# One transformer trunk layer on one core: softmax reciprocals spread as two fp16 parts, some weight high parts on GpSimd, and another written order of the attention stage

## The chip, the core and the metric

The kernel runs on one NeuronCore of one Trainium2 chip. A core has a matrix engine (TensorE, PE in the profile), a vector engine (VectorE, DVE), an activation engine (ScalarE, ACT), a general engine (GpSimd, POOL) and a queue engine that issues transfers (SyncE, SP). Each engine executes its own queue of instructions in order, and engines wait for one another through semaphores. The metric is device time in microseconds of one execution of the whole program; lower is better.

## The reference, cut to what matters

One trunk layer is computed for 128 context tokens and 512 latent tokens, with shared weights. All arithmetic of the reference is float32. Only the attention core is touched by the change:

```python
def block_attention(q, k, v):          # N queries, 16 heads of 64, 4 key/value heads
    ...
    s = jnp.einsum('bqkgd,btkd->bkgqt', qblk, k).astype(jnp.float32) * scale
    p = jax.nn.softmax(s, axis=-1).astype(v.dtype)
    return jnp.einsum('bkgqt,btkd->bqkgd', p, v)

def mixer(u, p, rope_tabs, ctx_k, ctx_v):
    z = u @ p["w_in"]
    ...                                 # split; RMS-normalise q and k per head, rotate latent ones
    att = block_attention(q_used, keys, vals) @ p["w_att_out"]
    conv = (b_gate * dwconv3(c_gate * x_in, p["conv_w"])) @ p["w_conv_out"]
    merged = jax.nn.sigmoid(g_att) * att + jax.nn.sigmoid(g_conv) * conv
    return merged @ p["w_o"], k, v
```

Context queries see the 128 context keys. Latent queries see 640 keys: 128 cached ones and the 512 latent ones. After the mixer come a residual with a norm, and a feed-forward part with 2 x 2816 columns.

## The kernel before

The program has a first part (modulation vectors, normalisation, key and value projections), the attention stage, and then the long dense products (attention output, gates, convolution mixer, feed-forward). Nearly all products are made from split operands: a matrix is cut into a high part and a low part, and three products (high by high, high by low, low by high) are summed. The high part of a weight block of 128 x 1024 is a copy on ACT (work `hi u`, L825), the low part is the difference of the block and its high part, in two halves of 512 columns on DVE or POOL (work `lo u`, L830).

The attention stage is what the change touches. It is not written as a loop. Its Python code first makes a list of works, small groups of instructions on one engine with the works they depend on and the buffers they need. Then `follow(PLAN)` emits them in the order of a long table of numbers. An item such as `67a0` says: work 67, its first way of being done (`a`; `b` and `c` are the same work on another engine), and buffer 0 for the buffer that it must choose. So the table sets the order of every engine's queue, which engine does a work that has two ways, and which buffer is used. Nothing is decided while the program runs; an engine whose next instruction is not ready waits, and all behind it wait too.

The works are these, with the lines under which the profile shows them:

- Query tiles. There are 20 of them, for 4 key/value groups `g` and 5 token tiles `t` (tile 0 is the context). A tile is projected in four pieces `q.0` to `q.3` on PE, each of six matmuls of 256 columns (L708). Then it is rotated on DVE (L848, L849; for the context L844), added on POOL or DVE (L869), squared on ACT (L871) and summed on DVE (L873); a factor is made by a power on POOL (L876) and applied on POOL (L891); PE turns it (L1033), and ACT and DVE cut it (L1035, L1037). Keys go through the same steps (L881, L920, L926, L929).
- Steps. There are 36: for each of the 4 groups one step of the context tile with four heads, and two steps for each of the four latent tiles, with two heads each. A latent step `n` consists of `s` (12 matmuls of scores on PE, L1072); for each of its two heads a maximum on DVE (`max`, L1119), for the second head a shift by a constant on DVE (L1122), the exponential with its row sum on ACT (`exp`, L1127), the fp16 high part of the result on ACT (`P1`, L1133), its low part on DVE or POOL (`P2`, L1138, L1140) and a transposing transfer issued by SP (`T`, L1144); a reciprocal of the two row sums on DVE (`inv`, L1146); and `pv` on PE. The work `pv` first spreads the reciprocals over a PSUM bank by an fp32 product with the identity (L1161, one matmul for each head, a row of 128 reciprocals repeated 64 times) and then multiplies values by probabilities (L1169, 30 matmuls of fp16).
- After the two `pv` of a tile: `R` copies the spread reciprocals to SBUF on ACT (L1181), `O` multiplies on DVE by these and by a factor of the value columns (L1185), and `AH` and `AL` cut the result for the next product (ACT L1188, DVE L1191).
- Gates: `gate0` and `gate1` on PE (L708 too), the last of them after the last scores.

The scores of a head lie in one of three PSUM areas. Where the string `POOL_WAY` has a 1 for a step, the exponential of its second head goes to an SBUF buffer `E` (two of them) and the low part is made on POOL; otherwise it stays in its PSUM area until DVE has made the low part.

The attention stage lies from about 57 to 229 us in the profile: its first matmuls of L708 start at 56.91, the first of the next product (L235, tile b) at 229.02.

Of the kernel before, what the change touches and what calls it, by code (L numbers as in the profile page):

```python
# [26 lines left out]
HD = 64  # L27
# [23 lines left out]
67a0 44a0 12a00 203a 24a1 137a 34a2 68a 25a 13a 0a 32a11 131a 2a1 69a 11a 26a 6a 3a 41a 33b 70a 14a1 35a 51a2 4a 1a3 79a1 53a4  # L51
71a0 15a 21a 80a 36a 5b0 31a 72a2 81a 45a 52a3 7a 16a 37b1 82a 22a12 92a2 46a 85a1 73a 8a0 23b 83a10 17a2 54a3 9a 86a 132a 38a1
10a 27a3 42a01 18a0 39a 93a 55a 19a 43a 40a 28a4 74a 60b2 94a 29a 59b3 95a 87a 75b 20a 105a3 98a0 84a 30a 76a1 106a 88a 77a0 99a
78a 107a 100a 58b4 56a0 47b4 65a 347a2 57a 134b 61a 96a22 48a1 63a 348a 108a 97a 49a 118a0 349a 101a 109a01 119a 133b 50a 89a2
102a1 120a 62a 90a1 209a 111a2 351a1 91a 110a 121a 112a 138a 66a 113a 359a10 352a 124a1 103a2 114a 122a10 204a 353a5 365a 140b
115a4 135a0 116a3 366a 104a 367a0 139b 136a 117a 350a 360a 368a0 373a20 123a 275a 125a 361a 64a 126a 141a 362a4 379a 205b 142a
380a 371a 363a 381a1 354a1 369a 143a2 364a0 382a2 374a 391a10 355a2 144a0 356a 383a 375a 151a0 370a1 145a 397a 357a 152a 376a1
146a 398a 385a 384a2 392a 399a0 153a 377a 147a 393a 154a 358a 206b 405a02 394a3 378a3 155a01 400a4 395a 127a 148a1 157a2 411a
401a 149a0 128a3 372a0 396a4 129a1 412a 158a 413a1 130a 159a 406a 414a0 423a12 403a 402a5 150a 407a 415a 164a1 429a 408a2 165a
156a 430a 281a 409a 431a0 166a 416a0 160a 424a 432a1 167a 417a 425a 433a 437a02 168a20 426a3 435a 386a 170a1 443a 169a 410a1  # L60
444a 427a 177a1 387a2 445a1 388a 178a 438a 389a 428a2 446a4 455a12 390a 171a 439a 447a 404a0 456a 440a0 434a3 449a 457a 441a
172a 418a 461a 458a2 173a 161a2 442a4 419a1 179a 459a 162a2 180a 163a 462a 420a 463a0 469a10 448a5 181a10 464a3 467a 182a 487a2
470a 183a0 421a 465a 190a1 460a0 488a 471a 191a 475a 472a1 192a 422a 210a 184a 466a1 174a0 473a 193a 185a 175a3 489a 176a 476a
186a 194a02 450a0 211a 436a 212a 477a1 474a4 490a 195a 478a0 481a 499a10 196a2 907a 479a 451a1 197a 207a1 491a4 505a 276a 208a
198a 506a 480a5 452a 507a0 492a 213a 199a 500a 453a 513a20 508a2 493a2 454a 278b 501a 468a0 514a 509a 502a3 519a 515a 214a 503a
277b 510a3 516a1 482a 520a 215a2 521a1 517a 187a3 504a0 483a0 511a 525a 531a02 188a1 484a 522a0 189a 518a1 200a3 216a1 523a 537a
485a 494a1 201a0 486a 538a 217a 223a0 495a2 202a 524a4 218a 539a0 496a 224a 532a 497a 219a 540a4 545a12 498a 533a 911a 541a
220a1 551a 534a2 225a 221a2 552a 226a 535a 542a5 553a1 546a 554a3 563a02 227a11 547a 555a 536a2 222a 548a1 557a 512a1 569a 229a0
228a 570a 549a 571a0 526a 556a0 564a 572a0 577a12 543a 230a 527a0 573a 565a 528a 550a3 236a0 583a 529a 566a4 231a 237a 575a 584a
# [19 lines left out]
880a0 885a 934a 840a 856a0 841a 895a 886a5 896a 842a 935a2 897a 890a 898a1 936a 891a 899a 937a 892a4 901a 900a2 938a 943a 893a  # L89
939a 894a4 940a 870a 888a1 871a2 872a 902a 873a 874a 941a 903a1 904a 942a 905a 906a  # L90
"""
POOL_WAY = "11111111111111111111111101111100"


def rope_tables():
# [17 lines left out]
def trunk_layer(ctx, tc, x_prompt, x_sample, cache_k, cache_v, c, c_ctx, w_ada, b_ada, g_pre1, g_post1, g_pre2,  # L113
# [632 lines left out]
    with tc.tile_pool(name="att", bufs=1) as at:  # L746
# [45 lines left out]
        def at_bank(room, n=512):  # L792
            return bank_of(room.at[0][1])[:, 0:n]
# [1594 lines left out]
```

## Time and profile before

| what | value |
|---|---|
| median of three runs | 1079.62 us (1079.02 to 1079.99) |
| the profiled execution's own time | 1079.34 us |
| its span in the profile | 1077.5 us |
| PE, DVE, ACT, POOL busy, whole span | 1062.8, 870.3, 583.1, 130.8 us |
| attention stage | 57 to 229 us |

"Busy" is time in which an engine has an instruction in flight. Instructions of one engine overlap a little, so the time from the start of one to the start of the next is often shorter than the duration that a row shows; for the queue of an engine it is the start-to-start time that counts. A row of a group reads: line, engine, operation, output<-inputs, shape, count | busy time, mean duration in ns | idle time of the engine before these instructions, and what ended it. A row of a timeline reads: start, busy time, engine, line, operation, count, and in brackets the idle time before with what ended it.

### The profile page before, as it was taken

To read this page: it belongs to the slowest core of one execution; us is meant where nothing else is said; L and a number is where in the kernel's file an instruction comes from. 1 tells how busy PE (TensorE), PEld (TensorE's weight loads), DVE (VectorE), ACT (ScalarE), POOL (GpSimd) and SP (SyncE) were. 2 spreads that over 40 slices of the span, in tenths; PEclk is the share of its full clock that TensorE was granted. 3 is DMA by queue.
4 is the path that set the end of the run, shared out by engine and by line. 5 is a ranking of instruction groups with operands and counts; after the bars stand their busy time and mean duration, and the time that the engine had idled before them with its cause. 6 is when DMAs were issued, how large, how long until landed. Compare 5 with 4: busy or idle time off the path is not lost.

```text
span 1077.5 us, 20246 instructions
## 1 busy us (share of the span) xinstructions
PE 1062.8 (99%) x8066; PEld 992.2 (92%) x8066; DVE 870.3 (81%) x1328; ACT 583.1 (54%) x1050; POOL 130.8 (12%) x162
## 2 busy tenths in 40 slices
PE   8999999999999999999999999999999999999997
PEld 6788898899999999999998789999999999998886
DVE  5699899855498999896599678889998998989544
ACT  5478999942344554445322466655555654555432
POOL 1087676500000000000000020000000000000001
PEclk9999999999999999999999999999999999999999
DMA  9829999962244333233667634333443443326722
GB/s 316 260 80 175 190 172 180 194 144 60 78 123 124 98 94 94 79 89 100 184 191 257 196 122 137 111 103 104 130 134 112 130 127 106 116 91 210 266 77 98
DMA packets 238444, 152.17 MB, mean 141 GB/s; under 512 B 94602, under 2 KB 215942, under 8 KB 238350
## 3 DMA queue, kind: packets, MB, share of 16 engines
q1 hardware_dynamic: 238238, 150.84, 51.6%
q8 instruction: 63, 1.03, 0.4%
q14 instruction: 31, 0.25, 0.1%
q10 hardware_dynamic: 112, 0.04, 0.0%
HBM read 117.39 MB, written 11.44 MB: 120 GB/s over the span
## 4 chain that ended last, share of the span: by engine, by line
PE 89%; DVE 3%; DMA 3%; ACT 2%; POOL 1%; issue 1%; SPq 0%; DVEq 0%; ACTq 0%; POOLq 0%
PE b L1273 47%; PE b L235 10%; PE b L237 10%; PE b L236 10%; PE s L708 3%; PE s L1072 2%; PE s L1169 2%; DMA araw<-in_w_ada_dram 1%; DMA PT<-P 1%; PE s L235 1%; PE s L237 1%; PE s L477 1%; DMA XT<-in_w_ada_dram 1%; DVE marks L1119 1%; ACT P L1133 1%
## 5 line engine op out<-in xcount | busy, mean ns | idle before, releaser
L1273 PE MATMUL b<-ZBr,whi 128*128 128x320 f32 x688 | 152.2, 309 | 0.0
L1273 PE MATMUL b<-MT,whi 128*128 128x320 f32 x608 | 134.3, 308 | 0.0
L1273 PEld LDWEIGHTS b<-ZBr,whi 128*128 128x128 f32 x688 | 115.0, 188 | 0.1
L1273 PE MATMUL b<-ZBr,wlo 128*128 128x320 f32 x344 | 106.2, 309 | 0.0
L1273 PEld LDWEIGHTS b<-MT,whi 128*128 128x128 f32 x608 | 101.6, 187 | 0.0
L1273 PE MATMUL b<-MT,wlo 128*128 128x320 f32 x304 | 93.6, 308 | 0.0
L1260 ACT ACTIVATE whi<-SUM 128x1024 fp32r<-128x1024 f32 x40 | 42.2, 1055 | 78.4 <-DVE SUM L1812 75.9
L1842 DVE SCALAR_TENSOR_TENSOR Y<-C,cffn,Y 128x642 f32<-128x642 f32 x88 | 77.6, 881 | 0.9
L201 DVE TENSOR_TENSOR wlo<-raw,whi 128x1024 fp32r<-128x1024 f32 (+1 forms) x31 | 34.2, 1102 | 48.2 <-ACT whi L200 47.8
L1273 PE MATMUL b<-ZBT,whi 128*128 128x320 f32 x320 | 71.0, 309 | 0.0
L1273 PE MATMUL b<-UL,whi 128*128 128x320 f32 x228 | 70.7, 310 | 0.0
L1273 PE MATMUL b<-UH,wlo 128*128 128x320 f32 x228 | 70.1, 307 | 0.0
L1260 ACT ACTIVATE whi<-WB 128x1024 fp32r<-128x1024 f32 x38 | 40.1, 1055 | 55.3 <-DVE WB L1367 55.3
L1273 PE MATMUL b<-UH,whi 128*128 128x320 f32 x228 | 69.8, 306 | 0.0
L1273 PEld LDWEIGHTS b<-ZBr,wlo 128*128 128x128 f32 x344 | 64.6, 188 | 0.0
L1281 ACT ACTIVATE p<-b 128x320 f32<-128x320 f32 x78 | 34.2, 438 | 55.5 <-PE b L1273 53.7
L1264 DVE TENSOR_TENSOR wlo<-raw,whi 128x1024 fp32r<-128x1024 f32 (+1 forms) x51 | 50.3, 1017 | 10.3 <-ACT whi L1260 10.3
L1273 PEld LDWEIGHTS b<-MT,wlo 128*128 128x128 f32 x304 | 57.0, 187 | 0.0
L1273 PEld LDWEIGHTS b<-ZBT,whi 128*128 128x128 f32 x320 | 54.2, 188 | 1.5
L1119 DVE TENSOR_REDUCE marks<-s 128x1 f32<-128x640 f32 x64 | 52.0, 816 | 4.1 <-PE s L1072 3.8
L1264 DVE TENSOR_TENSOR wlo<-WB,whi 128x1024 fp32r<-128x1024 f32 x38 | 46.4, 1222 | 8.7 <-ACT whi L1260 8.6
L2250 POOL TENSOR_TENSOR ssqs<-ssqs 128x1 f32<-128x1 f32 x4 | 0.8, 194 | 417.2 <-ACT JK L2243 417.2
(424 smaller groups left out, 3256.8 us busy)
## 6 DMA issues: line engine op xcount, KB each, us to landing
raw<-in_w_in_dram SPq DMA_DIRECT2D x48, 512.0 KB
RAW<-in_w_up_dram SPq DMA_DIRECT2D x40, 512.0 KB
raw<-in_w_down_dram SPq DMA_DIRECT2D x22, 512.0 KB
GA<-in_w_ada_dram SPq DMA_DIRECT2D x16, 512.0 KB
actd<-Y SPq DMA_DIRECT2D x18, 321.0 KB
XT<-in_w_ada_dram SPq DMA_DIRECT2D x9, 512.0 KB
raw<-in_w_att_out_dram SPq DMA_DIRECT2D x8, 512.0 KB
raw<-in_w_conv_out_dram SPq DMA_DIRECT2D x8, 512.0 KB
```

Source lines behind the costliest of these rows:

```text
L201: V.tensor_tensor(out=lo[:, :n], in0=raw, in1=hi[:, :n].bitcast(F32), op=ALU.subtract)
L235: PE.matmul(out, ah, bh, start=start, stop=False)
L236: PE.matmul(out, ah, bl, start=False, stop=False)
L237: PE.matmul(out, al, bh, start=False, stop=stop)
L708: PE.matmul(out, a, b, start=start and n == 0, stop=stop and n == 2, skip_group_check=True)
L1072: PE.matmul(o[h], q_of(hl, i, rows), kk[kx][rows, g, ks], start=m == 0, stop=m == 2, tile_position=(64 * h, 0), skip_group_check=True)
L1119: V.tensor_reduce(out=mk[:, h:h + 1], in_=s_of(), axis=AX.X, op=ALU.max, negate=True)
L1260: S.activation(to[0], raw, AF.Copy)
L1264: V.tensor_tensor(out=lo, in0=raw, in1=hi.bitcast(F32), op=ALU.subtract)
L1273: PE.matmul(out, p[:, ws], q[:, k, :], start=start and k == 0 and n == 0, stop=stop and k == 3 and n == 2, skip_group_check=True)
L1281: S.activation(t, pair[j][b], AF.Copy)
L1842: V.scalar_tensor_tensor(out=y, in0=crows(j)[i][:, d:d + NACT], scalar=cffn[:, 44 * d + o:44 * d + o + 1], in1=y, op0=ALU.mult, op1=ALU.add)
```

## The change

It has three parts.

1. The reciprocal spread. `inv` stays on DVE. Three small works follow it for each step, each on DVE or POOL as the table says: `ri` multiplies the two (context tile: four) reciprocals by a power of two, `rh` casts them to fp16 in a new tile `shares`, `rl` writes the rest as a second fp16 value. `pv` spreads them by two fp16 products with an fp16 identity for each head, summed in PSUM, where it had one fp32 product. The factor of the value columns becomes the same for both heads, so its tile `vcol` has four columns.
2. `hi u` gets a second way: on POOL, as a product with a column of ones. The table takes it for the weight blocks 16 and 17.
3. A new table `PLAN` (1052 items, before 944; 108 of them are new works) and a new `POOL_WAY` (30 steps with their low part on POOL, before 29; the last four latent steps before were 1100 and are 1111 now).

By the two tables the works with two ways are divided so:

| work | before | after |
|---|---|---|
| `ri`, `rh`, `rl` (36 each) | none | 14, 17, 16 on DVE; 22, 19, 20 on POOL |
| `hi` of a weight block | 9 on ACT | 7 on ACT, 2 on POOL |
| `lo` (half a block) | 5 DVE, 13 POOL | 7 DVE, 11 POOL |
| `P2` of latent steps | 35 DVE, 29 POOL | 34 DVE, 30 POOL |
| `add` of keys and queries | 4 DVE, 16 POOL | 5 DVE, 15 POOL |
| `norm` of keys | 3 DVE, 2 POOL | 1 DVE, 4 POOL |
| `v lo` | 3 DVE | 2 DVE, 1 POOL |

All other works stay on their engines. The counts of matmuls of the stage, of transfers and of the works of `max`, `exp` and `P1` do not change, but for the spread.

The diff, cut:

```diff
 PLAN = """
-67a0 44a0 12a00 203a 24a1 137a 34a2 68a 25a 13a 0a 32a11 131a 2a1 69a ...
+67a0 44a0 32a00 131a 14a1 203a 68a 12a11 24a2 33a 31a 137a 21a 25a 69a ...
 """
-POOL_WAY = "11111111111111111111111101111100"
+POOL_WAY = "10111111111111110111111111111111"
...
-        some = at.tile([128, 128], BF16, name="some")
+        lifts = at.tile([128, 4], F32, name="lifts")
+        some = at.tile([128, 2], BF16, name="some")
+        ident16 = at.tile([128, 128], F16, name="ident16")
+        shares = at.tile([128, 8, 8], F16, name="shares")
         G.memset(some, 1.0)
-        for i in range(2):
-            G.tensor_scalar(out=backs[:, i:i + 1], in0=ident[:, 0:1], scalar1=2.0 ** (SHIFT * i), scalar2=None, op0=ALU.mult)
+        G.memset(lifts, 2.0 ** (2 * SHIFT))
+        G.memset(lifts[:, 0:1], 2.0 ** SHIFT)
+        G.tensor_copy(ident16, ident)
+        G.tensor_scalar(out=backs, in0=ident[:, 0:2], scalar1=2.0 ** (2 * SHIFT), scalar2=None, op0=ALU.mult)
...
-                S.activation(made["x"][1], raw, AF.Copy)
+                if eng is S:
+                    S.activation(made["x"][1], raw, AF.Copy)
+                else:
+                    G.tensor_tensor(out=made["x"][1], in0=raw, in1=ones[:, 0:1].broadcast_to((128, 1024)), op=ALU.mult)
...
+        def parted(n, m, lift, mk, after):
+            sh = shares[:, n % 8, :]
+
+            def small(eng):
+                eng.tensor_copy(sh[:, 0:m], mk[:, 8:8 + m])
+
+            def rest(eng):
+                eng.tensor_tensor(out=sh[:, 4:4 + m], in0=mk[:, 8:8 + m], in1=sh[:, 0:m], op=ALU.subtract)
+            def lifted(eng):
+                eng.tensor_tensor(out=mk[:, 8:8 + m], in0=mk[:, 8:8 + m], in1=lift, op=ALU.mult)
+            a = work(f"inv{n}", "DVE", lambda: V.reciprocal(mk[:, 8:8 + m], mk[:, 4:4 + m]), after)
+            a = also(work(f"ri{n}", "DVE", lambda: lifted(V), [a]), "POOL", lambda: lifted(G))
+            a = also(work(f"rh{n}", "DVE", lambda: small(V), [a]), "POOL", lambda: small(G))
+            return also(work(f"rl{n}", "DVE", lambda: rest(V), [a]), "POOL", lambda: rest(G))
...
-                invs = [work(f"inv{n}", "DVE", lambda mk=mk: V.reciprocal(mk[:, 8:10], mk[:, 4:6]), exs)]
+                invs = [parted(n, 2, lifts[:, 0:2], mk, exs)]
...
                     for h in range(2):
-                        c = 8 + 2 * i + h if t == 0 else 8 + h
-                        PE.matmul(p[64 * h:64 * h + 64, 256 + 128 * i:384 + 128 * i], mk[:, c:c + 1].broadcast_to((128, 64)), ident,
-                                  start=True, stop=True, tile_position=(0, 64 * h), skip_group_check=True)
+                        for m in range(2):
+                            c = 4 * m + (2 * i + h if t == 0 else h)
+                            PE.matmul(p[64 * h:64 * h + 64, 256 + 128 * i:384 + 128 * i], sh[:, c:c + 1].broadcast_to((128, 64)), ident16,
+                                      start=m == 0, stop=m == 1, tile_position=(0, 64 * h), skip_group_check=True)
```

The order itself is shown at two places on which the prediction rests. The first is PE at an ordinary `pv`, a latent step. Before, the spread is one row of two fp32 matmuls (L1161; `marks` holds the reciprocals) ahead of the value products (L1169, with values `VV` and transposed probabilities `PT`):

```order
L1072 MATMUL s2_103_932<-KH_167,QT1_765 128x320
L1161 MATMUL s1_94_786<-ident_72,marks_771 64x128 x2
L1169 LDWEIGHTS VV_171
L1169 MATMUL s1_94_786<-PT4_753,VV_171 64x128
L1169 MATMUL s1_94_786<-PT5_754,VV_171 64x128
```

and of the change the same place, where the spread (L1191, the pair of rows stands four times: high and low part of the first head, then of the second) is of fp16, with its weights loaded from `shares`:

```order
L713 MATMUL s1_98_843<-whi_99_861,UL_95 128x256
L1191 LDWEIGHTS shares_778
L1191 MATMUL s1_94_791<-ident16_777,shares_778 64x128
L1199 LDWEIGHTS VV_171
L1199 MATMUL s1_94_791<-PT3_752,VV_171 64x128
L1199 MATMUL s1_94_791<-PT2_751,VV_171 64x128
```

The fp32 spread of two matmuls became four matmuls of fp16, and what stands behind it is the same.

The second place is the POOL queue around the steps 15 to 19 (`P` rows are the low parts of the second heads; `rq` rows are factors; `QF` rows add and norm; `wlo` rows low parts of weights). Before:

```order
L1138 TENSOR_TENSOR P1_745<-E0_742,P1_745 128x640
L1138 TENSOR_TENSOR P2_746<-E1_743,P2_746 128x640
L876 TENSOR_TENSOR rq_768<-ssqs_770,mhalf_81 128x4
L891 TENSOR_TENSOR QF2_763<-QF2_763,rq_768 128x256
L830 TENSOR_TENSOR wlo_118_2409<-raw_110_1343,whi_117_2408 128x512
L869 TENSOR_TENSOR QF1_762<-QF1_762,X1_759 128x256
L1138 TENSOR_TENSOR P1_745<-E0_742,P1_745 128x640
```

and of the change (L1167 are the low parts of the second heads, L890 a factor, L843 half a low part of weights, L1075, L1070 and L1073 are `ri`, `rh` and `rl`, L838 is the high part of weight block 16):

```order
L1167 TENSOR_TENSOR P3_747<-E0_742,P3_747 128x640
L843 TENSOR_TENSOR wlo_118_2257<-raw_110_1307,whi_117_2256 128x512
L1075 TENSOR_TENSOR marks_771<-marks_771,lifts_775 128x2
L890 TENSOR_TENSOR rq_768<-ssqs_770,mhalf_81 128x4
L1070 CAST shares_778<-marks_771 128x2
L1073 TENSOR_TENSOR shares_778<-marks_771,shares_778 128x2
L1167 TENSOR_TENSOR P2_746<-E1_743,P2_746 128x640
L838 TENSOR_TENSOR whi_120_2446<-raw_115_1595,ones_88 128x1024
```

Between two low parts (and after the last row of this piece one more `ri` and a factor, ahead of the next low part) there stand now small works that wait for reciprocals of DVE, and the high part of a block, where there stood factors, norms and halves of low parts of weights.

More of the change, by code (lines that the diff above doesn't have):

```diff
@@ L830, in lo @@
                 eng.tensor_tensor(out=l[:, a:b], in0=raw[:, a:b], in1=h[:, a:b].bitcast(F32), op=ALU.subtract)
-            h = work(f"hi {u}", "ACT", hi, [loaded["u", u], cut_of.get(u - 1)] + old)
+            h = also(work(f"hi {u}", "ACT", lambda: hi(S), [loaded["u", u], cut_of.get(u - 1)] + old), "POOL",
+                     lambda: hi(G))
             ls = [also(work(f"lo {u}", "DVE", lambda a=a: lo(a, a + 512), [h]), "POOL",
@@ L1093, in trunk_layer @@
                 exps_all.append(ex)
-                iv = work(f"inv{n}", "DVE", lambda mk=mk: V.reciprocal(mk[:, 8:12], mk[:, 4:8]), [ex])
+                iv = parted(n, 4, lifts[:, 1:2].broadcast_to((128, 4)), mk, [ex])
                 def p4(pr=pr):
```

99 lines of the change are left out of this document (52 added, 47 removed).

## The prediction

> **What bounds the kernel now.** I read the page first, then the attention stage by itself, then who waits for whom there, then the chain that ended last, and last the timelines of single engines. The page says that the program as a whole is a TensorE program at full clock:
>
> ```profile
> span 1077.5 us, 20246 instructions
> PE 1062.8 (99%) x8066; PEld 992.2 (92%) x8066; DVE 870.3 (81%) x1328; ACT 583.1 (54%) x1050; POOL 130.8 (12%) x162
> PE 89%; DVE 3%; DMA 3%; ACT 2%; POOL 1%; issue 1%; SPq 0%; DVEq 0%; ACTq 0%; POOLq 0%
> ```
>
> The change touches only the attention stage, and what follows it is dense PE work, so I let a gain or a loss of the stage go to the end one for one. The stage, cut at the starts of the scores of steps 5, 15, 25 and 35 and at its end (each busy time is followed by the count of instructions; after POOL come the clock, the DMA share and GB/s):
>
> ```profile
> 57.00:92.60 35.60, 33.41 (x337) 30.66 (x335) 34.08 (x80) 28.70 (x68) 34.15 (x34) 1.00 0.46 101
> 92.60:133.70 41.10, 39.71 (x582) 35.37 (x578) 36.73 (x81) 37.55 (x87) 26.65 (x26) 1.00 1.09 194
> 133.70:174.80 41.10, 41.07 (x570) 37.22 (x568) 38.03 (x87) 37.26 (x88) 27.55 (x26) 1.00 1.06 176
> 174.80:215.30 40.50, 39.43 (x607) 35.81 (x606) 35.29 (x78) 37.68 (x89) 21.79 (x19) 1.00 1.15 186
> 215.30:229.00 13.70, 13.38 (x197) 12.37 (x197) 6.92 (x14) 7.44 (x16) 0.00 (x0) 1.00 0.71 133
> sum 172.00, PE 167.00 PEld 151.43 DVE 151.04 ACT 148.63 POOL 110.13; mean PE 33.40 PEld 30.29 DVE 30.21 ACT 29.73 POOL 22.03
> ```
>
> The columns are PE, weight loads, DVE, ACT, POOL. PE leads with 167 of 172 us, but DVE (151) and ACT (149) are close behind, and POOL is full in the first stretch (34.15 of 35.6). So PE time saved here is not all time won. How much of it is, the chain tells. Its shares by line, from 57 to 150 us and from 150 to 232 us:
>
> ```profile
> by line: PE s L708 20.4%; PE s L1072 13.2%; PE s L1169 10.4%; POOL wlo L830 5.4%; DMA PT<-P 5.4%; POOL P L1138 4.5%; PE s L1161 4.0%; POOL rq L876 3.9%; issue 3.8%; DVE marks L1119 3.4%; PE s L1033 3.0%; DVE ssqs L873 2.6%; POOL QF L891 1.8
> by line: PE s L708 18.4%; PE s L1072 11.7%; PE s L1169 8.8%; issue 7.7%; ACT P L1133 7.7%; ACT s L1127 5.3%; DVE marks L1119 4.9%; DMA PT<-P 4.1%; PE s L1161 3.4%; DVE P L1140 3.0%; ACT E L1127 2.8%; SPq L1144 2.8%; DVE P L1138 2.0%; ACT s
> ```
>
> The spread of the reciprocals, L1161, stands there with 4.0% of 93 us and 3.4% of 82 us: 3.7 + 2.8 = 6.5 us.
>
> **The change, part by part.** *The spread on PE.* The timeline of PE has it, start in the first column:
>
> ```profile
> 161.13 0.66 PE L1161 MATMUL s<-ident,marks 128*64 128x128 f32 x8
> 161.62 0.51 PE L1169 MATMUL s<-PT,VV 128*64 128x128 f16 x12
> 175.95 0.44 PE L1161 MATMUL s<-ident,marks 128*64 128x128 f32 x4
> 176.22 1.01 PE L1169 MATMUL s<-PT,VV 128*64 128x128 f16 x30
> 177.05 0.39 PE L1161 MATMUL s<-ident,marks 128*64 128x128 f32 x4
> 177.27 1.01 PE L1169 MATMUL s<-PT,VV 128*64 128x128 f16 x30
> ```
>
> A latent spread (its two fp32 matmuls are four records) holds the queue from 177.05 to 177.27, 0.22 us; behind scores 0.27, where the 0.05 more belongs to the change of work and stays. A context spread holds it 0.49 us. That is 32 x 0.22 + 4 x 0.49 = 9.0 us, of which the chain's 6.5 are 0.7. The new fp16 spread is in no trace yet. Its nearest row is L1169, fp16 of the same shape: from 176.22 to 177.05 there are 30 matmuls, 0.028 us each, because the two heads lie on different columns and run in pairs of 0.056. Four such are 0.11 us if they pair. But the new order is both parts of head one, then both of head two (the front's rows): if the parts of one head follow each other and the heads overlap only in the middle, it is three times 0.056, 0.17 us. I take the middle, 0.14 (context: twice that). Saved: 32 x 0.08 + 4 x 0.21 = 3.4 us; ends 32 x 0.05 + 4 x 0.15 = 2.2 and 32 x 0.11 + 4 x 0.27 = 4.6. On the chain 0.7 of it: **-2.4 us** (ends -1.5 and -4.6, the latter if all lies on the path).
>
> [...]
>
> *The small works.* On DVE 47 are added. The rows of the trace nearest to them are reciprocals of two columns; on POOL, operations on one column; and beside them stand the other things that change engine:
>
> ```profile
> 208.38 0.22 DVE L1146 RECIPROCAL marks<-marks 128x2 f32<-128x2 f32 x2
> 208.51 0.81 DVE L1140 SCALAR_TENSOR_TENSOR P<-s,P 128x640 f16<-128x640 f32 x1
> 209.41 0.17 DVE L1146 RECIPROCAL marks<-marks 128x2 f32<-128x2 f32 x1
> L2250 POOL TENSOR_TENSOR ssqs<-ssqs 128x1 f32<-128x1 f32 x4 | 0.8, 194 | 417.2 <-ACT JK L2243 417.2
> L281 POOL TENSOR_SCALAR var<-ssq 128x1 f32<-128x1 f32 x5 | 1.5, 292 | 6.8 <-ACT junk L434 6.8
> L825 ACT ACTIVATE whi<-raw 128x1024 fp32r<-128x1024 f32 x9 | 9.6, 1065 | 0.0
> L830 POOL TENSOR_TENSOR wlo<-raw,whi 128x512 fp32r<-128x512 f32 x13 | 17.8, 1377 | 5.4 <-ACT whi L825 5.4
> L1138 POOL TENSOR_TENSOR P<-E,P 128x640 f16<-128x640 f32 x29 | 40.8, 1408 | 30.8 <-ACT P L1133 30.6
> ```
>
> Two reciprocals hold DVE's queue from 208.38 to 208.51, 0.065 us each; one that has its result awaited lasts 0.17. So 47 works are 3.1 to 8.0 us; I take 0.08 each, 3.8, since the new order mostly puts other work between. The works that change engine (front's table) take about 1.0 off DVE: one low part of 0.73 start to start and one of 0.6, two key norms of 0.6, one add of 0.33, against two halves of `lo` at 0.6 and two adds at 0.33 more for queries less one of keys. DVE: +2.8. DVE's lines are 4.9 + 3.0 + 2.0 = 10% of the chain above: **+0.3 us** (ends 0 and +2.8).
>
> ACT loses two high parts of 1.07, some 1.9 us start to start. Its lines L1133 and L1127 are 16% of the second chain: **-0.3 us**.
>
> POOL gets 61 small works at 0.2 to 0.3 (12 to 18 us; its one long small row, the power L876, is another function), two high parts of twice a half block, 2 x 2.5, one low part more (1.4), two halves of `lo` less (-2.5), and key norms, adds and `v lo`, +3: about +19 us, so 129 of 172. What hides it is this wait and the like, POOL idle for ACT:
>
> ```profile
> POOL P L1138 <- ACT P L1133: 30.6, 19, 3.5
> ```
>
> I cost it at nothing for that reason; without the cover it is the slower rival below. The setup on POOL (`lifts`, `ident16`) is of a few such small rows, ahead of the first norm, and falls in the same cover.
>
> *The order.* PE's longest waits at the start are for POOL's norms:
>
> ```profile
> 78.90 0.44 PE L1033 MATMUL s<-ident,QF 128*128 128x128 f32 x2 [0.77 <-POOL QF L891]
> 91.03 0.44 PE L1033 MATMUL s<-ident,QF 128*128 128x128 f32 x2 [1.06 <-POOL QF L891]
> ```
>
> The new table puts 36 query pieces ahead of the scores of step 5, before it was 28: 8 x 0.71 = 5.7 us of PE work that needs no norm, and as much less in later steps, where PE is the fullest engine. Price: from -1.8 (both waits go) to 0 (others come in their place); I take **-0.4**, since the first stretch stays full on POOL. The tail hardly moves. Before, the last transfer sets the last `pv`:
>
> ```profile
> 215.33 0.52 PE L1072 MATMUL s<-KH,QT 64*128 64x320 f32 x2
> 222.61 3.37 DMA PT<-P
> 226.02 1.03 PE L1169 MATMUL s<-PT,VV 128*64 128x128 f16 x30 [0.32 <-DMA PT<-P]
> ```
>
> Now the last two low parts go to POOL (1.41 against 0.82, +0.6 on the last transfer), and PE gets two more gate pieces between those scores and that `pv` (12 matmuls of 128 columns, 0.11 each, +1.3 of cover): nothing in sum.
>
> Sum: -2.4 + 0.3 - 0.3 - 0.4 = -2.8 us. The profiled execution took 1079.34 (span 1077.5 and 1.8 around it), 0.3 under the median of 1079.62; so 1076.5 for it, and **1076.8 us** against the median.
>
> **The rivals.** *Nothing measurable.* The spread leaves PE, and the time goes into waits for ACT and DVE, which alternate on the second chain (ACT 16%, DVE 10%, "issue" 8%). For it speaks that DVE gets busier by what PE gets freer; against it that PE has only 5.0 us of idle in 172. The time is then -2.4 turned into idle, 1079.2.
>
> *Slower, by POOL's queue.* POOL is in order, and now works that wait for DVE's reciprocals, and two high parts of 2.5 us, stand ahead of low parts. A late low part makes its transfer late, then `pv`, and holds a buffer `E`. Before a low part POOL had 30.6/19 = 1.6 us of slack where it waited. Three small works and their wait cost 0.6 to 1.0, a high part 2.5; it decides from where these exceed 1.6 in most steps. POOL's work can also stretch when DVE runs an operation with two inputs beside it:
>
> ```profile
> 153.06 0.69 DVE L830 TENSOR_TENSOR wlo<-raw,whi 128x512 fp32r<-128x512 f32 x1
> 153.10 1.80 POOL L830 TENSOR_TENSOR wlo<-raw,whi 128x512 fp32r<-128x512 f32 x1 [2.19 <-ACT whi L825]
> 158.58 1.29 POOL L830 TENSOR_TENSOR wlo<-raw,whi 128x512 fp32r<-128x512 f32 x1
> ```
>
> It took 1.80 beside one and 1.29 without. [...] If a third of the 19 us comes to the path, it is +6.3 - 2.8 = +3.5: 1083.1.
>
> *Faster still.* The new spread pairs, all 4.6 us of it lie on the path, and both starting waits go: -6.4 with ACT's 0.3 and DVE's 0.3 cancelling, 1073.2.
>
> **How the numbers follow.** Forecast 0.46, nothing 0.20, slower by POOL 0.22, faster still 0.12. A measurement can tell about 0.2%, 2.2 us, from no change. Of the forecast's case, whose own range is 1074.8 to 1078.4 (the spread's ends with the order's), 0.38 lies beyond 2.2 us and 0.08 within; of "nothing" 0.15 within and 0.05 above; of the slower one 0.03 within and 0.19 above. So faster 0.50, same 0.26, slower 0.24. The range goes from 1073.4, which leaves out half of the fastest case, to 1083.0, which leaves out half of the slower one.
>
> **What the profile after would show.** Right: the spread's four records from their start to the next row within 0.11 to 0.17 us; the stage's end (first L235 of tile b) at about 226; PE's idle in the stage still near 5 us; POOL near 129 us with shorter waits for ACT. Wrong: PE waiting for transfers or for `shares` written by POOL (the queue rival); PE idle grown by about 2.4 us with DVE above 154 (nothing); a spread that still takes 0.22 us, by which the main term would be gone.

## The result, and the profile after

The changed kernel takes 1086.33 us (median of 6 runs, 1085.24 to 1087.21), the kernel before beside it 1079.27 (6 runs, 1078.29 to 1079.99). The ratio is 1.0066, with a 95% interval of 1.0055 to 1.0078: slower by 7.1 us, where 2.8 us faster was forecast, and outside the range. The page after:

```profile
span 1084.9 us, 20343 instructions
PE 1061.5 (98%) x8066; PEld 988.8 (91%) x8066; DVE 883.2 (81%) x1374; ACT 583.2 (54%) x1048; POOL 144.9 (13%) x228
```

The first matmul of the product behind the attention stage, on PE's timeline before and now:

```profile
229.02 0.39 PE L235 MATMUL b<-AHa,whi 128*128 128x320 f32 x1
...
236.21 0.39 PE L240 MATMUL b<-AHa,whi 128*128 128x320 f32 x1
```

So the whole loss, 7.2 us, lies in the stage, and it went to the end one for one, as assumed (the span grew by 7.4). The stage of the changed kernel, cut at the scores of the same steps as before (5, 15, 25, 35); columns as in the table of before:

```profile
57.00:96.70 39.70, 38.08 (x353) 35.12 (x351) 37.94 (x91) 29.72 (x70) 35.48 (x42) 1.00 0.44 107
96.70:136.50 39.80, 38.50 (x593) 34.33 (x592) 38.23 (x90) 37.55 (x87) 30.66 (x47) 1.00 1.03 179
136.50:180.70 44.20, 40.11 (x564) 35.39 (x564) 41.65 (x97) 37.70 (x89) 30.35 (x45) 0.96 0.97 175
180.70:221.40 40.70, 35.88 (x571) 31.23 (x570) 38.12 (x89) 35.13 (x83) 24.01 (x30) 1.00 0.98 177
221.40:236.20 14.80, 14.16 (x209) 13.16 (x209) 7.46 (x17) 8.09 (x17) 3.48 (x6) 1.00 0.72 125
sum 179.20, PE 166.72 PEld 149.23 DVE 163.38 ACT 148.18 POOL 123.98; mean PE 33.34 PEld 29.85 DVE 32.68 ACT 29.64 POOL 24.80
```

PE's idle time rose from 5.0 to 179.2 - 166.7 = 12.5 us, and of it the waits that a DVE work ended rose from 2.3 to 9.7 us. DVE's busy time rose from 151.0 to 163.4, by 12.4 where the sum had 2.8. POOL's rose by 13.9, ACT's fell by 0.5. And the granted clock of PE, 1.00 in every stretch before, is 0.96 in the third.

**The spread did what it should.** On PE's timeline, start in the first column:

```profile
168.56 0.31 PE L1191 MATMUL s<-ident,shares 128*64 128x128 f16 x4 [0.23 <-DVE QF L863]
168.68 1.03 PE L1199 MATMUL s<-PT,VV 128*64 128x128 f16 x30
169.82 0.42 PE L1191 MATMUL s<-ident,shares 128*64 128x128 f16 x8
170.04 0.53 PE L1199 MATMUL s<-PT,VV 128*64 128x128 f16 x12
```

A latent spread holds the queue 0.12 us (168.56 to 168.68), a context one 0.22. That is the lower end of the price, the one for four products that run in pairs. Summed from start to start over the stage, with the few waits that fall into it, the spread takes 6.1 us, where it took 10.4.

**The small works on DVE did not.** DVE's groups in the stage (count, busy us and mean ns at the end):

```profile
...
L1073 DVE TENSOR_TENSOR shares<-marks,shares 128x2 f16<-128x2 f32 x12 | 5.3, 451 | 0.1
L1070 DVE CAST shares<-marks 128x2 f16<-128x2 f32 x15 | 5.1, 344 | 0.1
L1076 DVE RECIPROCAL marks<-marks 128x2 f32<-128x2 f32 x32 | 5.1, 158 | 2.0 <-ACT s L1156 1.8
L1151 DVE TENSOR_SCALAR marks<-marks 128x1 f32<-128x1 f32 x32 | 4.9, 152 | 0.8
L1075 DVE TENSOR_TENSOR marks<-marks,lifts 128x2 f32<-128x2 f32 x11 | 4.8, 433 | 0.3
...
L1114 DVE TENSOR_SCALAR marks<-marks 128x4 f32<-128x4 f32 x4 | 2.0, 502 | 0.1
```

Two columns take 0.16 us in a reciprocal, and 0.34 to 0.45 on average in the new works. The mean hides two kinds. Of the 47 new works 11 began beside a long POOL work (a low part, half a block or a high part) that had 0.48 us or more still to run. Each of the 11 lasted 0.50 to 1.75 us and ended 14 to 27 ns after it. Such a DVE work is called held from here on. The other 36 took 0.15 to 0.17, among them two that began in the last 0.06 and 0.11 us of a low part. The 11 make 10.3 us over 0.16 each. Eight reciprocals and 11 shifts of one column began and ended beside such POOL works, and none was held. What a hold does is seen in these rows of DVE, POOL, ACT and PE between 171 and 174.4 us (others between them are left out):

```profile
171.14 0.16 DVE L1076 RECIPROCAL marks<-marks 128x2 f32<-128x2 f32 x1
171.26 1.41 POOL L1167 TENSOR_TENSOR P<-E,P 128x640 f16<-128x640 f32 x1 [0.98 <-ACT P L1162]
171.33 1.35 DVE L1075 TENSOR_TENSOR marks<-marks,lifts 128x2 f32<-128x2 f32 x1
172.60 0.48 DVE L1215 SCALAR_TENSOR_TENSOR s<-s,vcol,X 128x256 f32<-128x256 f32 x1
173.12 0.39 ACT L1218 ACTIVATE AHb<-s 128x256 fp32r<-128x256 f32 x1 [0.89 <-DVE s L1215]
173.91 0.41 DVE L1221 TENSOR_TENSOR AL<-s,AHb 128x256 fp32r<-128x256 f32 x1
174.38 0.33 PE L1047 MATMUL s<-ident,QF 128*128 128x128 f32 x1 [1.61 <-DVE AL L1221]
```

`ri` starts 0.07 us after a low part on POOL and ends with it (172.68 against 172.67). `O` (L1215), `AH` and `AL` follow it, and PE waits 1.61 us for `AL`. Then this happens (the number behind POOL's is the granted clock of PE):

```profile
173.00:176.00 3.00, 1.39 (x12) 1.15 (x14) 3.00 (x8) 2.87 (x7) 0.52 (x3) 0.94 1.04 213
176.00:179.00 3.00, 3.00 (x17) 2.67 (x14) 2.73 (x7) 2.83 (x7) 2.48 (x4) 0.50 0.61 116
179.00:182.00 3.00, 2.90 (x29) 2.61 (x29) 1.93 (x8) 1.70 (x6) 2.73 (x5) 0.99 1.27 201
```

PE gets half its clock for 3.4 us, 1.7 us lost that no row shows as idle. Not all of the wait is the hold's. In the run told below that has all small works on POOL, the same matmul of PE waits for `AL` too, but less:

```profile
172.03 0.44 PE L1048 MATMUL s<-ident,QF 128*128 128x128 f32 x2 [0.51 <-DVE AL L1222]
```

So this hold of 1.2 us cost about 1.1 of the 1.61 us of idle. The half clock came behind it, but is not shown to be its price: in the run below with the high parts back on ACT, PE has the same wait of 1.61 us at 174.8 and keeps its clock.

The hold was in the trace of before, and the prediction does not have it. The shift of a context step's four maxima (L1085, in the changed kernel L1114) shows it beside the one-column shift (L1122):

```profile
L1122 DVE TENSOR_SCALAR marks<-marks 128x1 f32<-128x1 f32 x32 | 4.8, 151 | 0.8
...
L1085 DVE TENSOR_SCALAR marks<-marks 128x4 f32<-128x4 f32 x4 | 1.3, 324 | 0.1
```

The four took 0.17, 0.17, 0.40 and 0.56 us, and the two longer ones ended with POOL works that had begun before them. Of the works that were held in the changed kernel, `ri` and `rl` have two inputs in SBUF, `rh` is a cast, and the shift is a scalar operation on four columns. The traces show which forms are held; what holds them they do not show. The prediction weighed the two engines' works beside each other only with POOL as the one that is slowed (its low part of half a block took 1.80 us beside a DVE work with two inputs, 1.29 without).

### The profile page after: what moved, and what is told of

Read it like the earlier page. It is cut to its first block, busy times and chain, and to the rows that moved or that the text cites. A ratio compares the mean times of both kernels' runs of the same rounds, so it can differ in the third digit from the quotient of the medians.

```text
span 1084.9 us, 20343 instructions
## 1 busy us (share of the span) xinstructions
PE 1061.5 (98%) x8066; PEld 988.8 (91%) x8066; DVE 883.2 (81%) x1374; ACT 583.2 (54%) x1048; POOL 144.9 (13%) x228
## 4 chain that ended last, share of the span: by engine, by line
PE 79%; DVE 3%; ACT 1%; issue 0%; DMA 0%; SPq 0%; DVEq 0%; ACTq 0%
PE b L1303 47%; PE b L240 10%; PE b L242 10%; PE b L241 10%; DVE marks L1148 1%; PE s L713 1%; DVE P L1169 1%; PE b L1927 1%; PE s L1101 0%; PE b L1777 0%; ACT P L1162 0%; PE b L355 0%; DVE marks L1075 0%; DMA PT<-P 0%; DVE shares L1073 0%
```

## The experiments

Three theories were on record. *Held DVE*: the loss comes from small DVE works that last until a POOL work ends. *POOL's queue*: it comes from what now stands in POOL's order ahead of low parts, as in the prediction's slower rival. *The new order itself*: the table gives the time away. All times below are medians, against the kernel before on the same chip; the rows are from one profiled execution of each kernel.

**Where the small works are done.** First, all of them on POOL:

```diff
-... 375a ... 351a ... 353a ...      (ri, rh, rl: 47 items with way a)
+... 375b ... 351b ... 353b ...
```

> The changed kernel with all 108 small works (ri, rh, rl) on POOL, the order of the table kept. Three theories. (1) Held DVE: on DVE a small work with two SBUF inputs, or of two columns, does not end before the POOL instruction that is running; in the changed kernel's trace 11 of the 47 last 0.5 to 1.75 us, 10.4 us more than 0.16 each. With none on DVE these waits are gone: 1080 to 1082 us. (2) POOL's queue: small works that wait for DVE's reciprocals stand ahead of low parts; with 47 more of them there it is slower than the changed kernel, 1088 us or more. (3) The new order itself: nothing much changes, 1085 to 1087.

Measured 1081.32 against 1078.85, ratio 1.0025 (1.0016 to 1.0035). Of the 7.1 us 4.6 come back although POOL gets 47 works more: that is what held DVE gave, against POOL's queue. The profiled execution, with 1083.96 us the longest of the ten, shows one real wait for POOL, 1.6 us at 205 with half clock behind it:

```profile
PE s L1192 <- POOL shares L1074: 2.3, 2, 1.6
```

Second, the works stay on DVE, as one instruction for each column, with a constant or a pointer as second operand:

```diff
-                eng.tensor_copy(sh[:, 0:m], mk[:, 8:8 + m])
+                if eng is V:
+                    for c in range(m):
+                        V.tensor_scalar(out=sh[:, c:c + 1], in0=mk[:, 8 + c:9 + c], scalar1=1.0, scalar2=None, op0=ALU.mult)
...
-                eng.tensor_tensor(out=sh[:, 4:4 + m], in0=mk[:, 8:8 + m], in1=sh[:, 0:m], op=ALU.subtract)
+                if eng is V:
+                    for c in range(m):
+                        V.tensor_scalar(out=sh[:, 4 + c:5 + c], in0=sh[:, c:c + 1], scalar1=mk[:, 8 + c:9 + c], scalar2=-1.0,
+                                        op0=ALU.subtract, op1=ALU.mult)
...
```

> The changed kernel with its 47 small works of DVE written as one instruction for each column, with an immediate or a pointer scalar instead of a second SBUF tensor (twice the instructions); POOL's 61 as they are, the order kept. (1) Held DVE: the long ones shrink to 0.15 us, so most of the 7 us comes back: 1078 to 1081. (2) POOL's queue: what stands there is the same, 1085 to 1087. (3) The new order: 1085 to 1087.

Measured 1081.9, ratio 1.0029 (1.0019 to 1.0039), 0.9 above the expected range. Of 112 instructions, more than twice as many, none lasted over 0.22 us, though 41 of them began and ended beside a long POOL work. The shift of four columns (the last row), which this edit leaves as it is, was still held:

```profile
L1079 DVE TENSOR_SCALAR shares<-shares,marks 128x1 f16<-128x1 f16 x40 | 6.1, 206 | 0.0
L1072 DVE TENSOR_SCALAR shares<-marks 128x1 f16<-128x1 f32 x38 | 3.7, 146 | 0.0
L1086 DVE TENSOR_SCALAR marks<-marks 128x1 f32<-128x1 f32 x34 | 3.3, 147 | 0.3
L1128 DVE TENSOR_SCALAR marks<-marks 128x4 f32<-128x4 f32 x4 | 2.2, 546 | 0.1
```

Third, the two high parts go back to ACT:

```diff
-... 1016b ... 1020b ...
+... 1016a ... 1020a ...
```

> The changed kernel with the high parts of weight blocks 16 and 17 back on ACT, order kept. (1) Held DVE: one wait of 1.7 us (beside the high part of block 16) goes, ACT gets 1.9 us more: 1084.5 to 1086. (2) POOL's queue: 3.8 us of POOL go that stood ahead of low parts: 1082 to 1084. (3) The new order: 1086.

Measured 1086.71, ratio 1.0070 (1.0055 to 1.0085): nothing is gained. POOL's queue had 1082 to 1084, and held DVE missed too with 1084.5 to 1086; only the third theory had 1086. Against its own kernel before it is 0.8 us slower than the change (7.9 over, against 7.1), within the intervals.

**The order without the small works.** The new order, `POOL_WAY` and high parts on POOL, in the kernel before with its fp32 spread:

```diff
-PLAN, POOL_WAY of before
+PLAN of the change without the 108 items of ri, rh, rl; its POOL_WAY
-                S.activation(made["x"][1], raw, AF.Copy)
+                if eng is S:
+                    S.activation(made["x"][1], raw, AF.Copy)
+                else:
+                    G.tensor_tensor(out=made["x"][1], in0=raw, in1=ones[:, 0:1].broadcast_to((128, 1024)), op=ALU.mult)
```

> The new order, the new POOL_WAY and the two high parts on POOL, but the old fp32 spread and none of the small works. (1) Held DVE: the waits go, PE gets 4.7 us of spread back, most of it on the path: 1080 to 1084. (2) POOL's queue: the works that wait for DVE are gone, the high parts stay: 1080 to 1084 too. (3) The new order: at least as slow as the changed kernel, 1086 to 1091.

Measured 1083.75 against 1078.85, ratio 1.0045 (1.0030 to 1.0060), just inside the range of the first two theories. A loss of 4.9 us without any small work looks like the order, but DVE, POOL and PE at 187 us show a hold again, of the context shift, by the high part that the change put on POOL:

```profile
186.66 1.89 POOL L829 TENSOR_TENSOR whi<-raw,ones 128x1024 fp32r<-128x1024 f32 x1
186.81 1.77 DVE L1090 TENSOR_SCALAR marks<-marks 128x4 f32<-128x4 f32 x1
188.50 0.41 DVE L1196 TENSOR_TENSOR AL<-s,AHb 128x256 fp32r<-128x256 f32 x1
188.62 0.34 ACT L1096 ACTIVATE s<-s,marks 128x128 f32<-128x128 f32 x1 [1.25 <-DVE marks L1090]
...
188.96 0.70 PE L1166 MATMUL s<-ident,marks 128*64 128x128 f32 x4 [2.01 <-DVE AL L1196]
```

and then the clock:

```profile
185.00:188.00 3.00, 1.95 (x20) 1.54 (x19) 2.04 (x3) 1.84 (x5) 3.00 (x3) 1.00 1.11 209
188.00:191.00 3.00, 2.04 (x34) 2.01 (x34) 2.76 (x7) 2.25 (x9) 2.92 (x3) 0.58 0.10 22
```

**The shift in one-column form.** One edit, in three kernels: the run just told, all small works on POOL, and the one-column form.

```diff
-                    V.tensor_scalar(out=mk[:, 0:4], in0=mk[:, 0:4], scalar1=SHIFT * math.log(2), scalar2=None, op0=ALU.add)
+                    for c in range(4):
+                        V.tensor_scalar(out=mk[:, c:c + 1], in0=mk[:, c:c + 1], scalar1=SHIFT * math.log(2), scalar2=None, op0=ALU.add)
```

> The new order with the old fp32 spread and no small works (the run of e7), and one more edit: the shift of the four maxima of a context step, one DVE instruction on 128x4, is done as four instructions on one column. Held DVE: in e7 the shift of one context step lasted 1.77 us, from 186.81 to the end of the high part on POOL beside it (1.89 us), the low part AL stood behind it in DVE's queue, PE waited 2.01 us for AL, and then PE's granted clock was 0.50 for 3.4 us, which is 1.7 us lost. Without the hold this goes: 1080 to 1081, where e7 had 1083.75, and no stretch with the clock at 0.5. The order itself: the shift is one of many waits, and the time stays at 1083 to 1084. POOL's queue: nothing of it changes here, 1083 to 1084.

> The change with all 108 small works on POOL (the run of e1) and the context shift in four instructions on one column. Held DVE: the shifts of e1 took 1.5 us more than alone, one of the four next to the high part; the rest of e1's loss is a wait of PE for shares written by POOL (1.6 us at 205, with 1.7 us of half clock behind it), which stays: 1079.5 to 1081, where e1 had 1081.3. The order itself: as e1, 1081.3. POOL's queue: as e1, 1081.3.

> The change with DVE's small works in one-column form (the run of e2) and the context shift in the same form, so that nothing small on DVE can be held. Held DVE: 1.4 us of held shifts go, 1080 to 1081 where e2 had 1081.9. The order itself: 1082. POOL's queue: 1082.

Measured against 1078.61: 1081.36, ratio 1.0022 (1.0013 to 1.0031), for the first, 0.4 above the expected range, with the clock at 1.00 throughout the stage; 1080.15, 1.0017 (1.0008 to 1.0026); and 1079.98, 1.0015 (1.0006 to 1.0023). Each against its own kernel before, the three gain 2.2, 0.9 and 1.7 us by one edit. The last is the changed kernel with nothing small on DVE that can be held: 5.7 of its 7.1 us are gone.

**The old order.** Part 1 alone, with the small works right behind the reciprocal, on DVE in both forms:

```diff
-... 374a 366a ...                     (inv1 and a low part of step 1: the order before)
+... 374a 375a 376a 377a 366a ...      (ri1, rh1, rl1 behind inv1's item, and so for each step)
```

> Part one of the change alone: the order, POOL_WAY and high parts of before, with the fp16 spread and the three small works on DVE right behind each reciprocal (two columns, two SBUF inputs). PE saves 4.7 us of spread (0.11 a spread instead of 0.22, measured in the changed kernel). (1) Held DVE: 96 works of which a good half fall beside a long POOL instruction (POOL is busy 64% of the stage); the first of the three waits for its end, some 0.6 us on average: 36 x 0.64 x 0.6 = 14 us on DVE; slower than before, 1084 to 1092. (2) POOL's queue: none of them is on POOL, so the gain of the spread shows: 1076 to 1079. (3) The new order was the cause: 1076 to 1079 too.

> As the kernel with the old order and the small works on DVE, but written as one instruction a column without a second SBUF tensor: 6 instructions a step instead of 3, some 0.08 to 0.17 us each, 17 to 36 us... of which what depends on each other costs most. (1) Held DVE: no waits for POOL; 1077 to 1083, and clearly less than the two-column form of the same order. (2) and (3): like the two-column form or slower by the added instructions.

Measured 1111.29 against 1078.77, ratio 1.0303 (1.0278 to 1.0328), and 1094.57, 1.0151 (1.0134 to 1.0168): both far above what was expected. DVE's rows of the first:

```profile
L1071 DVE CAST shares<-marks 128x2 f16<-128x2 f32 x32 | 11.4, 358 | 1.1
L1074 DVE TENSOR_TENSOR shares<-marks,shares 128x2 f16<-128x2 f32 x32 | 11.3, 353 | 1.1
L1076 DVE TENSOR_TENSOR marks<-marks,lifts 128x2 f32<-128x2 f32 x32 | 10.6, 330 | 1.1
```

With the context steps the works take 34.4 us of DVE's queue, from start to start; 26 of them are held, by 19.3 us over 0.16 each. The time rose by 32.5. In one-column form none is held, the queue takes 24.2 and the time rises by 15.8. So the expectation for the second failed on a bare size: 240 instructions at 0.10 us. DVE has 21 us to spare in the stage of before (172 less 151), but evidently not where they are needed.

Idle DVE works in the kernel before measure small amounts: behind each latent reciprocal one product of two columns and two inputs, or one product of one column, that nobody reads.

```diff
+                    V.tensor_tensor(out=idle[:, 0:2], in0=mk[:, 4:6], in1=mk[:, 4:6], op=ALU.mult)
...
+                    V.tensor_scalar(out=idle[:, 0:1], in0=mk[:, 4:5], scalar1=1.0, scalar2=None, op0=ALU.mult)
```

> The kernel before with one idle instruction added on DVE behind each of the 32 reciprocals of latent steps: a product of two SBUF tensors of two columns that nobody reads. (1) Held DVE: those that fall beside a long POOL instruction (about 60%) last until it ends, 0.2 to 1.4 us; mean of the 32 above 0.4 us, and the time goes up by 3 to 8 us. (2), (3): they cost 0.08 us each, under 1 us in sum, the time stays within 1 us of before.

> The kernel before with an idle instruction at the same 32 places that reads one SBUF column and multiplies it by an immediate. (1) Held DVE: no waits, 0.15 us each by the profile, the time within 1 us of before. (2), (3): the same, so this run tells them apart only beside the one with two inputs.

Measured 1080.63 against 1078.77, ratio 1.0017 (1.0008 to 1.0027), 1.9 us and so below the expected 3 to 8, and 1079.08, 1.0004 (0.9995 to 1.0014), no difference that can be told from none. Of the first kind 8 of 32 were held, 3.2 us over 0.16 each:

```profile
L1149 DVE TENSOR_TENSOR idle<-marks 128x2 f32<-128x2 f32 x32 | 7.9, 246 | 0.0
```

So 3.1 us more in DVE's queue cost 0.3 us, 6.5 cost 1.9, 24.2 cost 15.8 and 34.4 cost 32.5: slack covers the first few.

Then the small works on POOL in the old order: right behind the reciprocal, and where POOL idled.

```diff
-... 374a 375a 376a 377a 366a ...
+... 374a 375b 376b 377b 366a ...      (all three on POOL, at the same place)
```

> Part 1 alone: the order before, the fp16 spread, and all 108 small works on POOL, right behind the reciprocal in the order. DVE gets nothing. Held DVE: no DVE work is added and the spread saves 4.7 us of PE, so faster than before as far as POOL lets it, 1075 to 1080. POOL's queue: small works stand there ahead of low parts without a written order made for them; each waits for a reciprocal of DVE, the low parts and their transfers are late, 1083 to 1090. The order itself: the old order is the better one, 1075 to 1077.

```diff
-... 374a 375b 376b 377b 366a ...
+... 374a 375a 376a 377a 366a ...      (step 1: on DVE, one-column form)
-...                                   (the other steps: on POOL, behind inv)
+...                                   (on POOL, ahead of the work before which POOL idled)
...                                    (and the one-column edits of DVE's small works and of the context shift, as above)
```

> Part 1 alone in the old order: the fp16 spread, the small works of 35 steps on POOL, each step's three works put ahead of that low part, factor or half block before which POOL idled in the trace of the kernel before, after the reciprocal's end and ahead of the spread (one step, whose works fit in no idle time, on DVE in one-column form), and the context shift in one-column form. Held DVE: no small DVE work can be held, POOL's works lie in its waits for ACT, so the spread's saving of 4.4 to 4.7 us shows, less about 1 us of small works in the full first stretch: 1074 to 1077. The order itself: the same, the old order is kept. POOL's queue: the works still make low parts late, as with all of them right behind the reciprocal: 1081 to 1084.

```diff
-... 374a 375a 376a 377a 366a ...
+... 383a 375b 376b 377b 147a ...      (step 1 on POOL too, ahead of a norm)
```

> As the run of e13, but the one step's works on POOL too, in the full first stretch ahead of a norm for which PE waits. Held DVE and the order itself: 0.5 us within e13, either way; POOL's queue: some 1 to 3 us slower than e13, since the norm is late by 0.7 us and a gap of PE can drop its clock.

Measured 1082.71 against 1078.61, ratio 1.0040 (1.0027 to 1.0053), for the first, between what held DVE (1075 to 1080) and POOL's queue (1083 to 1090) gave, close to the latter: POOL's queue is real there. PE waits for norms at the start, and gets half clock at 93:

```profile
PE s L1048 <- POOL QF L906: 4.0, 5, 1.5
```

With the works in POOL's idle time it is 1078.58 against 1078.75, ratio 0.9995 (0.9986 to 1.0004), the same as before; with one step more on POOL in the full first stretch 1079.98, 1.0013 (1.0004 to 1.0022), which is 1.4 us more. So three works of 0.2 us ahead of a norm for which PE waits cost 1.4 us; the profiled execution (1081.93) has again a stretch of half clock (at 94). But the first of the two was expected at 1074 to 1077. From 57 to 229 us its PE is busy 2 us less than before, and idles as much more:

```profile
sum 172.00, PE 164.94 PEld 149.27 DVE 151.43 ACT 149.19 POOL 128.46; mean PE 32.99 PEld 29.85 DVE 30.29 ACT 29.84 POOL 25.69
```

**What the spread and the order are worth.** To settle that, the fp16 spread takes a constant in place of the reciprocals, so that the kernel leaves out the small works and with them the normalisation of the attention, in the old and in the new order, both with the context shift in one-column form:

```diff
-                        PE.matmul(p[64 * h:64 * h + 64, 256 + 128 * i:384 + 128 * i], mk[:, c:c + 1].broadcast_to((128, 64)), ident,
-                                  start=True, stop=True, tile_position=(0, 64 * h), skip_group_check=True)
+                        for m in range(2):
+                            PE.matmul(p[64 * h:64 * h + 64, 256 + 128 * i:384 + 128 * i], evens[:, m:m + 1].broadcast_to((128, 64)), ident16,
+                                      start=m == 0, stop=m == 1, tile_position=(0, 64 * h), skip_group_check=True)
```

> The kernel before with the fp16 spread of two products for each head, but of a constant tile of ones in place of the reciprocals: the small works that make the two parts are left out, so the attention isn't normalised and the output isn't the reference's. The context shift is in one-column form. It shows what the 4.4 us that the spread leaves on PE are worth in the old order, at no price. Held DVE: the saving reaches the path nearly whole and the small works of e13 took it back, 1075 to 1076. Saving off the path (a rival that e13 raised: PE's time goes into waits for DVE and ACT, as the forecast's case of nothing measurable had it): 1077 to 1078.5. The order itself: 1075 to 1077.

> The same in the new order (the run of e10 with the fp16 spread of a constant tile): the small works are left out, and the output isn't the reference's. With e16 it gives the price of the new order and division, with nothing held and no small works. Held DVE: 1077 to 1078.5, 1 to 3 us above e16. Saving off the path: 1079 to 1081, within 1.5 us of e10. The order itself: 1079 to 1081, 4 us above e16.

Measured against 1078.89: 1078.03, ratio 0.9988 (0.9979 to 0.9997), and 1081.00, 1.0019 (1.0010 to 1.0028). The spread's 4.4 us on PE and the shift together are worth 0.9 in the old order, at no price: what the theory of a saving off the path gave, and not the 1075 to 1076 of held DVE. The new order costs 3.0 more, with no small works and no shift that can be held. In it PE waits for transposing transfers, which it hardly did in the old one:

```profile
PE s L1174 <- DMA PT<-P: 0.7, 1, 0.7
...
PE s L1179 <- DMA PT<-P: 4.2, 4, 1.4
```

Last, the one-column form of everything with the high parts back on ACT (the edit of the high parts above):

> The run of e12 (the change's order and division, nothing small on DVE that can be held) with the high parts of weight blocks 16 and 17 back on ACT, to see what part 2 is worth once it holds nothing. Held DVE: nothing is left that the two works of 1.9 us on POOL hold, so within 1 us of e12, 1079 to 1081. POOL's queue: they stand ahead of low parts, so 1 to 3 us faster, 1077 to 1079. The order itself: as e12.

Measured 1081.08 against 1078.75, ratio 1.0021 (1.0012 to 1.0030): 1.0 us more than with them on POOL, each against its own kernel before, at the edge of what held DVE gave, and no gain as POOL's queue had it; the intervals of the two overlap.

No version beats the kernel before by 0.2%: the best that computes the whole layer is level with it, and the one without any small work, 0.1% faster, bounds what part 1 can bring in the old order.

The 7.1 us are then, from these runs: spread and shift -0.9 (old order, constant); the new order and division +3.0 (new against old order, constant); the small works where none is held -0.7 (1.4 over before against 2.1 with the constant; the intervals overlap, so it may be nothing); the holds +5.7 (7.1 against 1.4). For the second entry no cause was tested. That late transfers are it is read from traces alone: in all six of the new order that have an edit to the one-column form PE waits 1.7 to 4.6 us for them, in the other four 0.6 to 1.2, in those of the old order at most 1.1.

## Why the prediction was wrong

- **The spread.** The fp16 price was 0.11 to 0.12 us, the best end of "0.11 to 0.17", and the saving 4.4 us, near the 4.6 of that end. The middle that the sum took, 0.14, was too much. The other reading of the order, in which the heads overlap only in the middle (three times 0.056), gave 0.17; the measured 0.12 decides against it. But "on the chain 0.7 of it" failed: 0.9 of 4.4 arrived, one fifth. The chain names PE for 0.7 of the spread's time because PE is last there; when PE gets faster, others become last. With the small works in POOL's idle time the waits of PE that a DVE work ended rose from 2.3 to 4.6 us. This is the mechanism of the rival "nothing measurable", and for part 1 in the old order it was right.
- **The small works on DVE.** This step failed most. "47 works at 0.08" priced them by reciprocals, a nearby form that was never held. 36 of them behaved so; 11 lasted 0.50 to 1.75 us. "DVE: +2.8" was 12.4, and "+0.3 us on the path" was about 4 of the 5.7 that the holds cost. So the size was wrong and the share too: a tenth was to be felt, by DVE's part of the chain, and about a third was. The other 1.7 or so is the context shift, which was no term of the sum at all (1.9 us between 1081.9 and 1079.98, each against its own kernel before: 3.1 and 1.4 us over it).
- **POOL.** "+19 us" was 13.9 in the stage (the high part took 1.90 us, not 2.5; the small works 0.19 to 0.20, as priced). "I cost it at nothing" was right about POOL's own queue: more work there made the kernel faster, and POOL's wait for ACT shrank from 30.6 to 20.1 us. It was wrong in what the cover means: POOL's work hides behind ACT, and in the meantime holds DVE. The contention was weighed in one direction only, POOL slowed by DVE.
- **The order.** "-0.4" was +3.0. The detail was right (PE's waits for norms at the start fell from 1.8 to 0.2 us) and the price wrong: as far as the traces show, waits for transfers came in their place later. Why these are late stays open.
- **ACT and the tail** were small, as said (-0.3 and 0 in the sum). With the high parts back on ACT the time is 0.8 and 1.0 us longer in the two runs that tried it, within their intervals, which has the sign of the -0.3; no run separates the tail.
- **The range.** The ends of the forecast's own case, "1074.8 to 1078.4", are not what its terms add up to: 1079.6 less 1.5 is 1078.1, and less 4.6 and 1.8 it is 1073.2. Nothing hangs on it, since the failed terms are others.
- **The slower rival** had the sign, with another mechanism. The runs that load POOL's queue (all small works there) and unload it (high parts back on ACT) speak against it in the change as it stands; in the old order, with the works right behind the reciprocal, it was true (+4.1 us).

## What to carry to other kernels

Before a short work goes to DVE, look in the trace at works of the same form (two SBUF inputs, casts, scalar operations on several columns) that ran beside long GpSimd works: if they end with those, price the new work by what GpSimd runs there, and use a form that was not held here (one column with a scalar, 0.13 to 0.21 us on average) or leave it on GpSimd. An engine's share of the chain of waits is no measure of what a change on it will be worth: here PE's seven tenths became a fifth of a gain, and of a loss on DVE, with a tenth of the chain, about one tenth was felt at 3 us more in its queue and nearly all at 34. A PE gap of 1.35 us and more was followed by half clock in some places and not in others, so count that as a risk beside the gap itself.

## What the runs showed of the hardware

- A DVE `TENSOR_TENSOR` with two SBUF inputs, a cast of two columns and a scalar operation on four columns that began beside a running POOL `TENSOR_TENSOR` other than the power with 0.43 us or more left lasted until its end in 13 of 13 cases of the changed kernel, two context shifts among them (0.45 to 1.75 us, where 0.15 to 0.17 is the time with nothing on POOL). Reciprocals of two columns (8) and scalar operations on one column (11) beside the long POOL works did not. In the traces of before and of the change together, with 0.3 us or more left, 15 of 15 works of the first kind lasted until POOL's end, and none of 19 reciprocals and 24 scalar operations on one column did; over all kept traces of the stage it was 78 of 78 (casts of four columns among them), and none of 201 and 515. POOL's power (L890, 1.07 us on average) held none: two small works began and ended beside it in the changed kernel, at 0.16 and 0.17 us.
- PE's clock fell to half for 3.4 us, 1.7 us lost, behind gaps of 1.60 (in two runs) and 1.61 us, behind one of 1.35 with another of 0.60 shortly before it, and inside one of 2.01 us after 1.5 us of it. It did not behind others of 1.60, 1.61, 1.84 and 2.25 us. In two runs of the old order it fell too: with the small works on DVE in two columns for 6.8 us from 86.5, inside a wait of 5.4 us and behind it, and for 3.4 us from 124.1; with the small works on POOL right behind the reciprocal for 3.4 us from 93.5, behind waits for norms of up to 1.5 us. What sets it off, these runs do not show.
